# First attention: probabilities scaled in place and transposed in one pass; and three changes of the second block

## Chip, core and metric

The kernel runs on one core of one Trainium2 chip. The time is the device time of one execution, in microseconds (us). TensorE (PE) multiplies matrices, VectorE (DVE), ScalarE (ACT) and GpSimd (POOL) do the rest, and SyncE (SP) issues most transfers.

## The reference, cut to what matters

Two transformer blocks run one after the other on 512 tokens of width 1024; the second puts 16 meta tokens in front (528 rows). Only the parts that the change touches are shown.

```python
# first block: attention over three dilations, 8 heads of 64
p = jnp.exp(s - m[..., None])
l = jnp.sum(p, axis=-1)
# out = sum_i e^{m_i} o_i / sum_i e^{m_i} l_i
# second block
proj = hn_p @ w_in[l]
sb_q, sb_k, sb_v, g_q, g_k, g_v, g_r, g_lr, merge = _split_cols(proj, IN_WIDTHS)
sb = _stick_breaking(...)   # z = q.k / sqrt(d), 8 heads of 64, blocks of 128 keys
glog = jax.nn.log_sigmoid((g_lr @ w_gk_up[l] + b_gk[l])) / GATE_TAU   # g_lr: 16 columns
h = h + _rmsnorm(mix, norm_mix_post[l])
hn = _rmsnorm(h, norm_ffn_pre[l])      # _rmsnorm: y = x * rsqrt(mean(x*x) + EPS) * g
```

## The kernel before

The first block keeps the tokens on the free axis. Its attention treats two heads at once (`hp`, four pairs) and four query blocks of 128 rows each (`i`); block `i` sees `i + 1` key blocks. A software pipeline of five stages runs over these 16 units: scores (`at_scores`), maximum and exponential (`at_exp`), transposition (`at_transpose`), copy out of PSUM (`at_evac`) and the product with the values (`at_out`, which also splits the finished pair of heads into a high and a low part on ACT and DVE, L220 and L221). `at_transpose` builds the diagonal of the reciprocal sums on ACT (L708) and multiplies the exponentials by it as a float32 product (L712), which scales and transposes them. A float32 product is two matmul instructions in the trace, a product of split operands (float32r) one, a transpose one.

Beside the attention DVE works off the taps of the causal convolution (`taps`, L635), which stand at a lower priority. Behind the attention PE does the first half of the output projection (`pw`); the convolution's result `y` is completed at L861 and enters the sums of `conv_norm` (L824). Memory that the attention held becomes the buffers `raw2`; the last columns of `w_mod` are loaded there, and GpSimd multiplies two of these loads (L519).

The weights come through one stream (`ws`): a unit is loaded into a `raw` buffer, and units that are marked for it are split into a high part (ACT, L220) and a low part (DVE or GpSimd, L221). Products of split operands are three matmuls (`mm3`, L309 to L311, and L1587, L1609, L2210).

At the start of the second block DVE and ACT make the normed input `nh`/`nl` (L1655 to L1657). The gate's rank-16 projection (`w_lr`, in the pool `pl`) is one unit of 128 columns of which 16 are used; ACT copies the result to `glr` (L1718), and `decay` multiplies it by `wgk`. Then one `weave` interleaves the stick-breaking attention (`sb_gen`), the projections of queries and keys (`qk_gen`), the gated attention (`gla_gen`) and a value projection. `sb_gen` is a pipeline over 40 units (pair of heads, key block `j`, head `b`) with the stages `sb_z`, `sb_soft`, `sb_cum`, `sb_sum`, `sb_exp`, `sb_out`; a score lies in its PSUM bank `pz` from `sb_z` to `sb_exp`. All of these streams take their banks from one pool of eight.

Behind the mixing, the class `Sums` adds up squares over the channels with products by ones, for the halves `a` of the tokens: 8 squares of the mixed output (`mix_mm`, `mix_out`) and 8 of the new residual (`h_gen`, for the feed-forward part's norm). Before, each square is multiplied by a 32-column piece of ones into one of four column groups, and `rstd` copies the four partial sums out (L1640) and joins them by one more product (L1641) ahead of the logarithm (L1642).

The order of instructions on each engine is decided when the program is built, by a planner that goes by priorities and by its own estimate of durations; `high_priority` and `keep_in_program_order` steer it. A change of one stage can so move instructions of others.

Of the kernel before, what the change touches and what calls it, by code (L numbers as in the profile page):

```python
# [11 lines left out]
F32 = mybir.dt.float32  # L12
F32R = mybir.dt.float32r
I32 = mybir.dt.int32
AF = mybir.ActivationFunctionType
# [5 lines left out]
P = 128  # L21
T = 512
D = 1024
KD = D // P
# [28 lines left out]
def pack_inputs(a):  # L53
# [18 lines left out]
    def cols(w, starts):  # L72

        kk = w.shape[0] // P
        return np.stack([w[:, s:s + P].reshape(kk, P, P).transpose(1, 0, 2).reshape(P, -1) for s in starts])
# [6 lines left out]
    def pair(x):  # L82
# [7 lines left out]
    w2 = f("w_in_2")[0]  # L90
# [14 lines left out]
                           .reshape(NE, 2, P, 2048) for w in (gate, up, down)], axis=1).reshape(NE, 6, P, 2048),  # L105
        "b_r": np.concatenate([f("b_router_group").reshape(1, 4), f("b_router_expert").reshape(1, NE)], axis=1),
        "w_v2": pair(np.concatenate([rows(w2[:, c:c + 512], 2) for c in (1024, 2560, 3072)])),
        "w_lr": cols(w2, [4608]),
        "w_qk2": pair(cols(w2, [c + h * P for c, h in (
            (0, 0), (512, 0), (1536, 0), (2048, 0), (1536, 1), (2048, 1), (0, 1), (512, 1),  # L110
            (1536, 2), (2048, 2), (1536, 3), (2048, 3), (0, 2), (512, 2), (0, 3), (512, 3))])),
# [84 lines left out]
def _build(ctx, nc, tc, I, out, dbg):  # L196
    mm = nc.tensor.matmul
    transpose = nc.tensor.transpose
    act = nc.scalar.activation
# [117 lines left out]
    big = A.enter_context(tc.tile_pool(name="A", bufs=1, side="right"))  # L317
# [11 lines left out]
    ident = const.tile([P, P], F32, name="ident")  # L329
    ones = const.tile([P, P], F32, name="ones")  # L330
    nc.vector.memset(ones, 1.0)
    epsb = const.tile([P, 1], F32, name="epsb")
# [42 lines left out]
    def p1(name="p1"):  # L375
        return pp.tile([P, 512], F32, name=name, tag="p1", bufs=4)
# [9 lines left out]
    plan = []  # L386
# [71 lines left out]
    nmoe = len(plan)  # L458
    two = (1024, 1024)
    plan += [(I["w_v2"][i], two, "keep") for i in range(2)]  # L460
    plan += [(I["w_lr"][0], (1024,), True)]
    plan += [(I["w_qk2"][i], two, True) for i in range(8)]
    plan += [(I["w_v2"][i], two, "keep") for i in range(2, 6)]
    plan += [(I["w_gr"][i], two, True) for i in range(4)]
# [11 lines left out]
    ws = Stream(plan, castp, 3, nmoe)  # L476
# [57 lines left out]
    for k in range(KD):  # L534
        sq = big.tile([P, T], F32, name="sq", tag=("sq", "t512")[k % 2], bufs=2)
# [4 lines left out]
        g = slice(32 * (k % 4), 32 * (k % 4) + 32)  # L540
# [161 lines left out]
    def at_transpose(un, st):  # L702
        hp, i = un
        s, sm = st
        nc.vector.reciprocal(sm[:, 6:8], sm[:, 4:6])
        dg = big.tile([P, 2, P], F32, name="dg", tag="dg", bufs=2)
        for b in range(2):
            act(dg[:, b, :], ident, AF.Copy, scale=sm[:, 6 + b:7 + b])  # L708
        pt = [p1("pt0"), p1("pt1")]
        for b in range(2):  # L710
            for j in range(i + 1):
                mm(pt[b][:, j * P:(j + 1) * P], s[:, b, j * P:(j + 1) * P], dg[:, b, :], start=True, stop=True)  # L712
        return pt

    def at_evac(un, pt):
# [713 lines left out]
    ws = main  # L1429
# [132 lines left out]
    def t5(name, p=P):  # L1562
        return HP.tile([p, L], F32, name=name, tag="t5", bufs=4)
# [15 lines left out]
    def proj2_gen(k, xh, xl, ps):  # L1579

        wh, wl = ws.nxt(P)
        for kk in range(k):
            if kk:
                yield
            for l, r, fl in ((wh, xh, 0), (wh, xl, 1), (wl, xh, 2)):
                for a in range(2):
                    mm(ps[a], l[:, kk, :], r[kk][:, a * HF:(a + 1) * HF],  # L1587
                       start=(kk == 0 and fl == 0), stop=(kk == k - 1 and fl == 2))
# [27 lines left out]
    def part(ap, a):  # L1616
        return ap[:, E[a][0]:E[a][1]]

    class Sums:
# [9 lines left out]

        def flush(self, a):  # L1630
            for sq in self.pend[a]:
                g, k = self.n[a] % 4, self.n[a]
                mm(self.ps[a][32 * g:32 * g + 32], ones[:, 0:32], part(sq, a), start=(k < 4), stop=(k >= 4),
                   skip_group_check=True)
                self.n[a] += 1
            self.pend[a] = []

        def rstd(self, a, r, count):
            ev = t5("ev")
            act(part(ev, a), self.ps[a], AF.Copy)  # L1640
            mm(self.ps[a], ones, part(ev, a), start=True, stop=True)  # L1641
            tc.keep_in_program_order(act(part(r, a), self.ps[a], AF.Ln, bias=epsb, scale=1.0 / (32 * count)))  # L1642
            tc.keep_in_program_order(act(part(r, a), part(r, a), AF.Exp, scale=-0.5))


# [63 lines left out]
    sv = sp_.tile([P, 5, 512], F32, name="sv")  # L1709
    sv_last = vproj_end(sv, psv[:4], psv[4], t5("tail")[:, :T], psx, rcol)  # L1710
    pl = [p("pl")[:, :HF] for p in (pns, psx)]
    for i, _ in enumerate(proj2_gen(KD, nh, nl, pl)):
        if i == 2:
            sv_last()
    tc.keep_in_program_order(nc.scalar.preload_act_table_set("natural_log_exp_and_others"))
    glr = t5("glr", 16)
    for a in range(2):
        act(glr[:, a * HF:(a + 1) * HF], pl[a][0:16], AF.Copy)  # L1718
    ws.lo = tt
    PB.close()  # L1720
    PS, p1, p2 = psum_pool("psumC", 4, 2)
    wgk = cp.tile([16, 512], F32, name="wgk")
    nc.gpsimd.dma_start(wgk, I["w_gk_up"])
    resetm = cconst("resetm", L)
    cum = s8("cum")

# [43 lines left out]
    def need(*what):  # L1770
        while not made.issuperset(what):
            next(qkg)
# [7 lines left out]
    def sb_keys(j):  # L1780
        return NM if j == 4 else P

    def sb_z(un, _):
        hp, j, b = un
        need(("s", hp))
        s0, t0, n = SBT[j]
        ps = p1("pz")
        r, p = slice(64 * b, 64 * b + 64), sb_keys(j)
        mm(ps[:p, :n], skh[hp][r, s0:s0 + p], sqh[hp][r, t0:t0 + n], start=True, stop=True)  # L1789
        return ps  # L1790

    def softplus(pss, n, p=P):

# [355 lines left out]
    def mix_mm(m, a):  # L2149
        if m not in wo:  # L2150
            wo[m] = ws.nxt(P)
            sqo[m] = t5("sq")
        wh, wl = wo[m]
        ps = pso[m, a] = p1("pmix")[:, :E[a][1] - E[a][0]]
        for kk in range(KD):
            mm3(ps, wh[:, kk, :], wl[:, kk, :], part(mh[kk], a), part(ml[kk], a), kk == 0, kk == KD - 1)

    def mix_out(m, a):
        ps = pso.pop((m, a))
        act(part(mx[m], a), ps, AF.Copy, scale=cc("norm_mix_post", m))  # L2160
        act(part(sqo[m], a), ps, AF.Square)
        su.add(a, sqo[m])

    for m in range(KD - 2):
        for a in range(2):
            mix_mm(m, a)
        for a in range(2):
            mix_out(m, a)
            if m in (3, 5):
                su.flush(a)  # L2170

    for a in range(2):
        for m in (KD - 2, KD - 1):
            mix_mm(m, a)
            mix_out(m, a)
        su.flush(a)
        with tc.high_priority(offset=100):
            su.rstd(a, r, D)
# [8 lines left out]
    def h_gen(a):  # L2187
        for k in range(KD):
            with tc.high_priority(offset=200):
                t, h, g = cp.tile([P, T], F32, name="t", tag="y", bufs=3)[:, :E[a][1] - E[a][0]], part(hT[k], a), cc("norm_ffn_pre", k)  # L2190
                tt(t, part(mx[k], a), part(r, a), OP.mult)
                (nc.gpsimd.tensor_tensor if k in HPL else tt)(h, h, t, OP.add)
                act(part(nh[k], a), h, AF.Copy, scale=g)
                stt(part(nl[k], a), h, g, part(nh[k], a).bitcast(F32), OP.mult, OP.subtract)
            sq = t5("sq")
            act(part(sq, a), h, AF.Square)
            su.add(a, sq)
            if k % 2:
                su.flush(a)
            yield  # L2200

# [159 lines left out]
```

## Time and profile before

| | us |
|---|---|
| timed runs | 1836.7, 1839.62 (median), 1840.88 |
| the profiled execution | 1838.8 |
| its span, first to last instruction | 1837.0 |
| PE busy | 1752.8 (95%) |
| DVE busy | 923.4 (50%) |
| ACT busy | 626.5 (34%) |
| POOL busy | 180.4 (10%) |

The busy shares are a mean over stages with different limits; the time of a stage is set by the engine that is busy throughout it, or by a wait. PE's busy time counts matmuls whose ends are modelled, and neighbours overlap.

### The profile page before, as it was taken

How to read it: one execution, taken by the hardware profiler on the slowest of the kernel's cores; microseconds unless marked ns; L12 is line 12 of the kernel's file. 1: busy time of each engine (PE TensorE's matmuls, PEld its weight loads, DVE VectorE, ACT ScalarE, POOL GpSimd, SP SyncE). 2: the span in 40 equal slices, each digit the busy share in tenths (PEclk: the TensorE clock that was granted, in tenths of full speed). 3: DMA queues.
4: the chain of work that ended last, by engine and by line, in shares of the span. 5: the costliest groups of instructions: out<-in, count | busy, mean ns of one | idle time of the engine just before them, and what ended most of it. 6: DMA issues, size and time to landing. Idle time of an engine off the chain costs nothing.

```text
span 1837.0 us, 26718 instructions
## 1 busy us (share of the span) xinstructions
PE 1752.8 (95%) x10738; PEld 1264.7 (69%) x10738; DVE 923.4 (50%) x1593; ACT 626.5 (34%) x1146; POOL 180.4 (10%) x162
## 2 busy tenths in 40 slices
PE   6978987999999999999999999999999999999997
PEld 4755754544445444445888768989999799889985
DVE  7999864542424343335577752253331654335534
ACT  3324653211111111104566663252223633223322
POOL 4541020000000000004100000030000111001101
PEclk9998998999999999999999999999999999999998
DMA  8743163899999999941411012113222122232221
GB/s 300 283 165 134 73 231 127 303 409 409 408 411 377 371 407 409 413 166 38 157 63 47 25 38 101 47 50 136 104 95 91 46 92 93 90 105 93 92 86 63
DMA packets 73889, 328.29 MB, mean 179 GB/s; under 512 B 7971, under 2 KB 8227, under 8 KB 59556
## 3 DMA queue, kind: packets, MB, share of 16 engines
q1 hardware_dynamic: 72608, 320.75, 46.3%
q0 software_dynamic: 1152, 5.81, 0.9%
q8 instruction: 85, 1.39, 0.3%
q14 instruction: 40, 0.33, 0.1%
q10 hardware_dynamic: 4, 0.00, 0.0%
HBM read 322.27 MB, written 4.26 MB: 178 GB/s over the span
## 4 chain that ended last, share of the span: by engine, by line
PE 50%; DVE 2%; ACT 1%; POOL 1%; issue 0%; DVEq 0%; ACTq 0%; POOLq 0%
PE p L1609 11%; PE pup L2210 7%; PE pq L1587 6%; PE pg L311 2%; PE pg L309 2%; PE pg L310 2%; PE pd L310 2%; PE pd L311 2%; PE pd L309 2%; PE pz L1789 1%; PE pv L309 1%; PE psb L1870 1%; PE pv L311 1%; PE pv L310 1%; PE pmix L309 1%; PE pmix L310 1%
## 5 line engine op out<-in xcount | busy, mean ns | idle before, releaser
L221 DVE TENSOR_TENSOR wsplit<-raw,wsplit 128x1024 fp32r<-128x1024 f32 (+1 forms) x140 | 166.8, 1194 | 258.5 <-ACT wsplit L220 253.0
L220 ACT ACTIVATE wsplit<-raw 128x1024 fp32r<-128x1024 f32 (+1 forms) x145 | 147.9, 1022 | 261.8 <-PE pd L311 76.4
L1195 PE MATMUL pgu<-raw,x 128*64 128x512 f32 x960 | 220.3, 598 | 0.0
L1195 PEld LDWEIGHTS pgu<-raw,x 128*64 128x64 f32 x960 | 64.1, 136 | 120.0 <-issue 106.9
L1288 DVE SCALAR_TENSOR_TENSOR x<-psx,modc,x 128x512 f32<-128x512 f32 x136 | 93.1, 744 | 48.1 <-PE psx L1296 48.0
L1237 DVE SCALAR_TENSOR_TENSOR yl<-pdn,wsl,yh 128x512 fp32r<-128x512 f32 x34 | 25.4, 751 | 178.8 <-ACT yh L1236 178.4
L1195 PE MATMUL pdn<-raw,hT 128*64 128x512 f32 x480 | 105.7, 593 | 0.7 <-ACT hT L1217 0.7
L635 DVE SCALAR_TENSOR_TENSOR y<-u,cpk,y 128x512 f32<-128x512 f32 x116 | 103.3, 924 | 0.4
L1217 ACT ACTIVATE hT<-pht 128x512 f32<-128x512 f32 x17 | 10.2, 598 | 232.1 <-PE pht L1211 227.5
L1195 PEld LDWEIGHTS pdn<-raw,hT 128*64 128x64 f32 x480 | 34.5, 137 | 69.1 <-issue 64.4
L310 PE MATMUL pd<-wsplit,ah 128*128 128x512 f32 x176 | 71.0, 403 | 2.1 <-DVE wsplit L221 2.0
L1157 PE MATMUL psg<-oh,h2h 128*128 128x256 f32 (+1 forms) x288 | 68.9, 297 | 3.2 <-DVE oh L1142 3.2
L311 PE MATMUL pd<-wsplit,al 128*128 128x512 f32 x176 | 70.0, 398 | 0.0
L309 PE MATMUL pd<-wsplit,ah 128*128 128x512 f32 x176 | 69.1, 398 | 1.0 <-ACT wsplit L220 1.0
L1609 PE MATMUL p<-nha,wsplit 128*128 128x258 f32 x384 | 68.6, 291 | 1.0 <-ACT grb L2059 0.6
L1157 PE MATMUL psg<-oh,h2l 128*128 128x256 f32 (+1 forms) x288 | 65.7, 281 | 0.0
L1609 PE MATMUL p<-nhb,wsplit 128*128 128x258 f32 x384 | 65.5, 282 | 0.0
L221 POOL TENSOR_TENSOR wlo<-raw,whi 128x1024 fp32r<-128x1024 f32 x20 | 59.4, 2982 | 57.7 <-ACT whi L220 47.2
L2210 PE MATMUL pup<-nha,wsplit 128*128 128x258 f32 x352 | 63.9, 290 | 0.9 <-ACT wsplit L220 0.9
L523 DVE CUSTOM_DVE_ANT_0 raw<-raw,h 128x1024 f32<-128x1024 f32 x38 | 62.4, 1668 | 1.1 <-DMA raw<-w_mod 1.1
L1295 PE MATMUL psx<-ohT,yh 128*128 128x512 f32 x136 | 59.3, 436 | 3.3 <-ACT uh L1455 3.0
L2210 PE MATMUL pup<-nhb,wsplit 128*128 128x258 f32 x352 | 61.4, 284 | 0.0
(649 smaller groups left out, 4050.7 us busy)
## 6 DMA issues: line engine op xcount, KB each, us to landing
raw<-w_moe SPq DMA_DIRECT2D x312, 512.0 KB, 10.1
raw<-w_moe SPq DMA_DIRECT2D x36, 1024.0 KB, 8.9
raw<-w_mod SPq DMA_DIRECT2D x24, 1024.0 KB, 6.4
raw<-w_ff SPq DMA_DIRECT2D x22, 1024.0 KB, 4.8
raw<-w_qk SPq DMA_DIRECT2D x12, 1024.0 KB, 4.9
raw<-w_v SPq DMA_DIRECT2D x8, 1024.0 KB, 4.9
raw<-w_mg SPq DMA_DIRECT2D x8, 1024.0 KB, 4.8
raw<-w_fd SPq DMA_DIRECT2D x8, 1024.0 KB, 4.8
```

What stands on the lines that cost most here:

```text
L220: act(hi, src, AF.Copy)
L221: return sub(lo, src, hi.bitcast(F32), OP.subtract)
L309: mm(ps, lh, rh, start=first, stop=False)
L310: mm(ps, lh, rl, start=False, stop=False)
L311: mm(ps, ll, rh, start=False, stop=last)
L635: tap[0] = stt(y[:, m, :], src, w, y[:, m, :], OP.mult, OP.add)
L1157: fix(mm(ps[k // 2][:, k % 2 * 256:][:, :n], w[i][:, k * P:(k + 1) * P], oh[:, i, :n], start=(i == 0 and w is h2h and k % 2 == 0), stop=(i ...
L1195: fix(mm(ps[s, :], l[:, s], w[:, 2 * b + i, :], start=first, stop=last, skip_group_check=True))
L1288: stt(xT[m], ps, gt2(m), xT[m], OP.mult, OP.add)
L1587: mm(ps[a], l[:, kk, :], r[kk][:, a * HF:(a + 1) * HF], start=(kk == 0 and fl == 0), stop=(kk == k - 1 and fl == 2))
L1609: mm(ps[a], l[:, kk, :], ends(r[kk])[:, a], start=(kk == 0 and fl == 0), stop=(kk == k - 1 and fl == 2))
L2210: mm(ps[:, a, :HC], l[:, kk, :], x[kk][:, o:o + HC], start=(kk == 0 and fl == 0), stop=(kk == KD - 1 and fl == 2))
```

## The change

Four edits. The probabilities are scaled in place on ACT and then transposed by PE's transpose instead of multiplied by a diagonal. The rank-16 projection loads 32 columns per 128 rows (16 used, 16 zero) without a split and runs as float32 products in four column groups; the four partial results are kept, and `wgk` holds the 16 rows four times, with zeros between, so that the decay product adds them up. The two heads' scores of a key block are issued together. `Sums` multiplies by the full square of ones, one square at a time and one step later, so that nothing has to be joined.

```diff
@@ pack_inputs
-        "w_lr": cols(w2, [4608]),
+        "w_lr": np.pad(w2[:, 4608:4624], ((0, 0), (0, 16))).reshape(KD, P, 32).transpose(1, 0, 2).reshape(1, P, KD * 32),
@@ the stream's plan
-    plan += [(I["w_lr"][0], (1024,), True)]
+    plan += [(I["w_lr"][0], (KD * 32,), False)]
@@ at_transpose
-        dg = big.tile([P, 2, P], F32, name="dg", tag="dg", bufs=2)
+        n = (i + 1) * P
         for b in range(2):
-            act(dg[:, b, :], ident, AF.Copy, scale=sm[:, 6 + b:7 + b])
+            act(s[:, b, :n], s[:, b, :n], AF.Copy, scale=sm[:, 6 + b:7 + b])
...
-                mm(pt[b][:, j * P:(j + 1) * P], s[:, b, j * P:(j + 1) * P], dg[:, b, :], start=True, stop=True)
+                transpose(pt[b][:, j * P:(j + 1) * P], s[:, b, j * P:(j + 1) * P], ident)
@@ Sums
             for sq in self.pend[a]:
-                g, k = self.n[a] % 4, self.n[a]
-                mm(self.ps[a][32 * g:32 * g + 32], ones[:, 0:32], part(sq, a), start=(k < 4), stop=(k >= 4),
-                   skip_group_check=True)
+                mm(self.ps[a], ones, part(sq, a), start=(self.n[a] == 0), stop=(self.n[a] == KD - 1))
...
         def rstd(self, a, r, count):
-            ev = t5("ev")
-            act(part(ev, a), self.ps[a], AF.Copy)
-            mm(self.ps[a], ones, part(ev, a), start=True, stop=True)
-            tc.keep_in_program_order(act(part(r, a), self.ps[a], AF.Ln, bias=epsb, scale=1.0 / (32 * count)))
+            tc.keep_in_program_order(act(part(r, a), self.ps[a], AF.Ln, bias=epsb, scale=1.0 / count))
@@ the rank-16 projection
-    for i, _ in enumerate(proj2_gen(KD, nh, nl, pl)):
-        if i == 2:
+    w = ws.nxt(32)
+    for k0 in (0, 4):
+        for x in (nh, nl):
+            for a in range(2):
+                for k in range(4):
+                    mm(pl[a][32 * k:32 * k + 32], w[:, k0 + k, :], x[k0 + k][:, a * HF:(a + 1) * HF].bitcast(F32),
+                       start=(k0 == 0 and x is nh), stop=(k0 > 0 and x is nl), skip_group_check=True)
+        if k0 == 0:
             sv_last()
...
-    wgk = cp.tile([16, 512], F32, name="wgk")
-    nc.gpsimd.dma_start(wgk, I["w_gk_up"])
+    wgk = cp.tile([P, 512], F32, name="wgk")
+    nc.gpsimd.memset(wgk, 0.0)
+    for g in range(0, P, 32):
+        nc.gpsimd.dma_start(wgk[g:g + 16], I["w_gk_up"])
@@ sb_z
+        if b == 0:
+            need(("s", hp))
+            s0, t0, n = SBT[j]
+            p = sb_keys(j)
+            for h in range(2):
+                pz[h] = p1("pz")
+            for h in range(2):
+                r = slice(64 * h, 64 * h + 64)
+                mm(pz[h][:p, :n], skh[hp][r, s0:s0 + p], sqh[hp][r, t0:t0 + n], start=True, stop=True)
+        return pz.pop(b)
@@ mixing
         for a in range(2):
             mix_mm(m, a)
+            su.flush(a)
         for a in range(2):
             mix_out(m, a)
-            if m in (3, 5):
-                su.flush(a)
...
         for m in (KD - 2, KD - 1):
             mix_mm(m, a)
+            su.flush(a)
             mix_out(m, a)
@@ h_gen
             act(part(sq, a), h, AF.Square)
+            su.flush(a)
             su.add(a, sq)
-            if k % 2:
+            if k == KD - 1:
                 su.flush(a)
```

## Rows read from the trace of the kernel before

**Rows 1.** Windows of the first attention, of what follows: engines' busy us, clock, DMA.
```profile
168.00:221.70 53.70, 46.14 (x358) 34.06 (x354) 49.75 (x131) 38.01 (x116) 1.56 (x1) 0.94 0.12 41
222.00:240.00 18.00, 12.59 (x42) 7.65 (x41) 17.20 (x13) 5.59 (x10) 9.65 (x3) 0.95 0.84 335
```

**Rows 2.** Timeline behind the attention: start, us, engine, line, operation, idle before it.
```profile
222.05 0.69 DVE L221 TENSOR_TENSOR ml<-pso,mh 128x512 fp32r<-128x512 f32 x1 [2.22 <-ACT mh L220]
226.15 6.50 DVE L635 SCALAR_TENSOR_TENSOR y<-u,cpk,y 128x512 f32<-128x512 f32 x3
226.47 4.84 POOL L519 TENSOR_TENSOR raw<-raw,u 128x2048 f32<-128x2048 f32 x1 [47.83 <-DMA raw<-w_mod]
241.37 2.08 PE L824 MATMUL psl<-y,ones 128*128 128x512 f32 x2 [6.78 <-DVE y L861]
```

**Rows 3.** Window of the stick-breaking and gated attention: PE, PEld, DVE, ACT, POOL.
```profile
896.00:1064.00 168.00, 166.67 (x1876) 130.92 (x1876) 114.92 (x251) 112.31 (x253) 4.17 (x8) 0.99 0.14 47
```

**Rows 4.** Timeline of PE: products with a diagonal; four transposes elsewhere, the next matmul.
```profile
188.56 2.05 PE L712 MATMUL pt<-dg,s 128*128 128x128 f32 x16
...
265.40 0.66 PE L806 MATMUL pth<-ident,xs 128*128 128x128 f32 x4
265.82 0.48 PE L309 MATMUL pw<-mh,whi 128*128 128x512 f32 x1
```

**Rows 5.** Groups by line and shape, 144 to 222 us: busy, mean ns, idle before.
```profile
L635 DVE SCALAR_TENSOR_TENSOR y<-u,cpk,y 128x512 f32<-128x512 f32 x69 | 51.0, 766 | 0.2
...
L708 ACT ACTIVATE dg<-ident,sm 128x128 f32<-128x128 f32 x32 | 11.1, 393 | 5.1 <-DVE sm L705 3.3 <-DVE sm L697 1.8
...
L699 ACT ACTIVATE s<-s,sm 128x512 f32<-128x512 f32 x8 | 5.7, 712 | 4.3 <-DVE sm L697 4.3
```

**Rows 6.** Timeline of the norm and the rank-16 projection at the second block's start.
```profile
868.37 2.41 POOL L221 TENSOR_TENSOR wsplit<-raw,wsplit 128x1024 fp32r<-128x1024 f32 x1 [0.15 <-ACT wsplit L220]
869.18 3.98 DVE L1657 TENSOR_TENSOR nla<-nt,nha 128x512 fp32r<-128x512 f32 x4
...
878.85 0.69 DVE L1657 TENSOR_TENSOR nlb<-nt,nhb 128x512 fp32r<-128x512 f32 x1
...
881.23 0.65 ACT L1718 ACTIVATE glr<-pl 16x264 f32<-16x264 f32 x2 [1.30 <-PE pl L1587]
...
883.40 2.36 DVE L221 TENSOR_TENSOR wsplit<-raw,wsplit 128x1024 fp32r<-128x1024 f32 x2
```

**Rows 7.** Score products: their busy time in one window (PE, PEld), then the timeline.
```profile
896.00:1064.00 168.00, 26.40 (x80) 9.99 (x80) 0.99 0.14 47
...
918.50 0.94 PE L1789 MATMUL pz<-sqk 64*128 64x400 f32 x2
...
937.42 1.12 PE L1789 MATMUL pz<-sqk 64*128 64x512 f32 x2
938.47 0.51 PE L1587 MATMUL pq<-nhb,wsplit 128*128 128x264 f32 x2
...
1059.97 0.94 PE L1789 MATMUL pz<-sqk 64*128 64x400 f32 x4
...
1062.31 1.56 PE L1789 MATMUL pz<-sqk 64*128 64x512 f32 x4
```

**Rows 8.** Sums of squares: windows (partial sums alone; all engines), then PE's timeline.
```profile
1396.00:1456.00 60.00, 14.27 (x64) 3.39 (x64) 0.94 0.16 53
...
1426.00:1436.00 10.00, 7.20 (x23) 3.13 (x22) 9.03 (x22) 8.38 (x21) 2.80 (x3) 0.68 0.00 0
...
1420.55 0.67 PE L1641 MATMUL psum<-ev,ones 128*128 128x260 f32 x2
...
1421.17 0.28 PE L309 MATMUL pmix<-mhb,wsplit 128*128 128x256 f32 x1
...
1428.93 0.62 PE L1633 MATMUL psum<-sq,ones 128*32 128x256 f32 x2 [1.86 <-ACT sq L2161]
1430.02 1.22 PE L1641 MATMUL psum<-ev,ones 128*128 128x256 f32 x2 [0.47 <-ACT ev L1640]
```

More of the change, by code (lines that the diff above doesn't have):

```diff
@@ L1711, in _build @@
     pl = [p("pl")[:, :HF] for p in (pns, psx)]
-    for i, _ in enumerate(proj2_gen(KD, nh, nl, pl)):
-        if i == 2:
+    w = ws.nxt(32)
[6 more added lines that the diff above has]
+        if k0 == 0:
             sv_last()
     tc.keep_in_program_order(nc.scalar.preload_act_table_set("natural_log_exp_and_others"))
-    glr = t5("glr", 16)
+    glr = t5("glr")
     for a in range(2):
-        act(glr[:, a * HF:(a + 1) * HF], pl[a][0:16], AF.Copy)
+        act(glr[:, a * HF:(a + 1) * HF], pl[a], AF.Copy)
     ws.lo = tt
@@ L1781, in sb_keys @@
         return NM if j == 4 else P
+    pz = {}
     def sb_z(un, _):
         hp, j, b = un
[L1785 to L1790, printed above, removed]
+        if b == 0:
[8 more added lines that the diff above has]
+        return pz.pop(b)
     def softplus(pss, n, p=P):
```

## Prediction

> **What bounds the kernel now.** A saving on TensorE (PE) counts only in a stage that waits for PE, so I read the busy time of all engines by window first, then the timeline at the places where PE stands still.
>
> In the first attention it is not PE. From 168 to 221.7 us VectorE (DVE) is busy 49.75 of 53.70 us, and 17.20 of 18.00 us behind it [rows 1]. It does the attention's reductions and, between them, the convolution taps. Past the attention PE stands 6.78 us until DVE has finished the convolution (L861) [rows 2]. Whatever PE does sooner in the attention is added to that wait, except for time in which DVE itself had nothing to do: 53.70 - 49.75 = 3.95 us in the attention and 0.80 us behind it. The longest piece is 2.22 us, the wait for the last head's output (L221 on ACT) [rows 2].
>
> In the second block it is PE: 166.67 of 168 us busy in the stick-breaking and gated-attention stage, with DVE at 114.92 and ACT at 112.31 [rows 3]. There a PE saving is a time saving as long as other matmuls are ready.
>
> **Part 1, probabilities.** Removed: 160 matmul instructions against a diagonal (4 head pairs, 10 blocks, 2 halves, each float32 product two instructions). Sixteen took 2.05 us, 0.128 each, so 20.5 us. Added: 80 transposes. Four transposes began at 265.40 and the next matmul at 265.82 [rows 4], 0.105 each, so 8.4 us. PE loses 12.1 us of work. ACT: 32 diagonals of 393 ns (11.1 us busy together) become 32 in-place scalings. For 128 columns I price them at the same 393, for 512 at the exponential's 712 [rows 5], between by a line (499, 606): 8 x 2.21 = 17.7 us, so ACT gains at most 6.6 us on 38.01 busy of 53.70 [rows 1] and stays below DVE. DVE's work is unchanged. So 12.1 us go off PE and at most 3.95 + 0.80 = 4.75 us come out. I take -2.5: the wait of 2.22 for the last head goes, little else. Bounds: -4.75, and +3, if the taps are ordered worse around the two GpSimd products that follow. While one of these runs (4.84 us from 226.47) three taps take 6.50 us [rows 2], against 766 ns for a mean tap [rows 5]; both products hit DVE wherever the taps stand, and a third one caught would cost some 4.2 us, less the 1 to 2 us of idle recovered.
>
> **Part 2, the gate's rank-16 projection.** Removed: 48 matmuls, and the split of their weight on ACT and GpSimd. Added: 32 float32 products of 32 columns, four at a time in four column groups. But the stage follows a norm chain on DVE: the last piece of its input (L1657) is made from 878.85 to 879.54, and the products end at 881.23, where ACT copies them [rows 6]. So the end moves by two small terms. First, the GpSimd split of this weight (868.37 to 870.78) overlaps four subtractions on DVE that take 3.98 us; at the 0.69 of the one that stands alone they would take 2.76 [rows 6], and 1.2 us go. Second, behind the last piece come two of the eight groups of four products; half a microsecond for a group is an estimate from a full-array float32 product of 260 columns (0.50, part 4), since the four run side by side: 1.0 instead of the 1.7 there now. Sum -1.9. Against it: the first product of the next projection needs a weight half that DVE splits from 883.40 on [rows 6], behind six other updates, and that moves only with the first term. I take -1.4, bounds 0 and -3. The added memset and three DMA issues stand on GpSimd's queue ahead of the reset mask; the first decay that reads it comes more than 10 us later, which hides them, and without that cover they cost their length, some 2 us.
>
> **Part 3, score pairs.** The 40 score products are 80 instructions, 26.40 us busy [rows 7]. Each uses 64 of the 128 rows, and 36 of them stand alone in the stream; only the last head's two largest pairs stand together (0.94 and 1.56 us). So 23.9 us are singles. A single of 512 columns is 1.12 us busy, but the next matmul begins 1.05 behind its start (937.42, 938.47): 0.07 of each is overlap, and 36 singles hold PE for 23.9 - 36 x 0.07 = 21.4 us. A pair of 400 columns takes 0.94 us, a single of 400 columns also 0.94 [rows 7]: the second half is free. So half of 21.4 goes, 10.7 us. PE has other matmuls in hand there, and DVE and ACT are at 67 to 68% [rows 3], so I take -9; bounds -10.7 and -3, the rest for banks (below).
>
> **Part 4, sums of squares.** Removed: four copies (ACT) and four products that joined the four partial sums. The 32 partial sums (14.27 us busy; with four joins of 0.67, 17.0) become 32 full-array products [rows 8]. A join of 260 columns is such a product: it begins at 1420.55, and the matmul after the next one at 1421.17, one slot of 0.12 after 1421.05, so it holds PE for 0.50. 32 x 0.50 = 16.0, so -1.0 on PE; with the busy time of a partial sum (0.45) it is -2.7, with that of a join (0.67) +4.4. More lies in one place: from 1426 to 1436 PE is busy 7.20 of 10.00 us at a mean clock of 0.68 [rows 8]. It waits 1.86 us for a square, then the join waits 0.47 for the copy and takes 1.22 at the lower clock. Without copy and join some 1.7 us of that chain go, and about 1 us of the same chain one half earlier. I take -2.7 there and -3.7 together; bounds -7 and +1.7.
>
> **The sum.** -2.5 - 1.4 - 9 - 3.7 = -16.6. The profiled execution took 1838.8 us (span 1837.0 and 1.8 around it), 0.8 below the median of the three timed runs, 1839.62. 1838.8 - 16.6 = 1822.2; I say 1822.
>
> **Rivals.**
> *Banks run out (slower).* A pair takes both its PSUM banks one unit early, and eight banks serve scores, projections and outputs. If PE's next instruction is a second score without a bank, it waits for the exponential of a unit four steps back, and all that is queued behind it on PE waits too. A step lasts 168 / 40 = 4.2 us; half a step at 18 pairs is 38 us, against 10.7 saved: 1838.8 - 7.6 + 27 = 1858. It turns to a loss once a pair waits 0.6 us. For it: five scores would be held at the peak instead of four. Against it: PE idles only 1.3 us in the stage now [rows 3], and two pairs already stand together. [...]
>
> [...]
>
> *The second block gives half.* Its filler is not ready, or ACT sets the pace of the last head: parts 2 to 4 give -7 rather than -14.1, the time is 1838.8 - 9.5 = 1829.
>
> **How the numbers follow.** Forecast 0.70, half 0.12, clock 0.10, banks 0.08. The forecast's own range, from the bounds of the parts, is 1812 to 1831; the range reaches to the half and the clock case and leaves the banks out: 1812 to 1833. A measurement of this kernel can tell 0.2%, 3.7 us. Faster by more than that: forecast, half, and less than half of the clock case (partly worse than worked out), 0.86; within it 0.06; slower: the banks, 0.08.
>
> **What would show it.** Part 1 right: DVE as busy as now up to the end of the convolution, PE's wait there longer than 6.78 us, the convolution done 2 to 3 us sooner; wrong: DVE idle more, or L861 later. Part 2: the products end about 1 us behind the last DVE subtraction. Part 3: 20 groups of four score instructions with about half of 26.40 us, and no new waits before them; a wait for an exponential in front of a score is the bank rival. Part 4: no copy and no join, and the low-clock stretch between mixing and feed-forward shorter by 2 us. [...]

## The result, and the profile after

The changed kernel takes 1827.45 us, the median of 6 runs (1825.18 to 1828.79); the kernel before took 1838.13 in as many runs on the same chip. The ratio is 0.9942, with a 95% interval of 0.9930 to 0.9953: 10.7 us faster. The prediction was 1822, with a range of 1812 to 1833. The profiled execution took 1827.8 us (span 1826.0 and 1.8 around it), 11.0 below that of before.

Where these 11.0 us come from is read from PE's timeline, from one landmark to the next: the first product of `psk` (L1018, behind the router), the last transpose of `pht` (L1211, the end of the experts), the first product of `pq` (L1587, behind the rank-16 projection), the first transpose of `pkt` (behind the stick-breaking and gated attention), and the end of the span.

| stage, us | before | after | difference | part |
|---|---|---|---|---|
| start to `psk` | 314.0 | 314.4 | +0.4 | 1 |
| `psk` to last `pht` | 507.0 | 506.2 | -0.8 | none |
| last `pht` to `pq` | 62.7 | 62.5 | -0.2 | 2 |
| `pq` to `pkt` | 241.0 | 233.9 | -7.1 | 3 |
| `pkt` to the end | 712.3 | 709.0 | -3.3 | 4 |

First the windows of the changed kernel that answer to [rows 1] and [rows 3] (PE, PEld, DVE, ACT, POOL busy, granted clock, DMA):

```profile
168.00:221.70 53.70, 42.77 (x298) 26.52 (x295) 48.40 (x130) 41.83 (x113) 1.56 (x1) 0.94 0.14 42
222.00:240.00 18.00, 13.04 (x45) 7.97 (x43) 17.20 (x14) 6.52 (x10) 10.28 (x3) 1.00 0.94 386
896.00:1064.00 168.00, 163.48 (x1907) 130.89 (x1908) 122.15 (x266) 117.75 (x274) 10.39 (x18) 0.98 0.14 48
```

In the attention PE is relieved, DVE is idle for 5.30 us where it was 3.95, and ACT has grown from 38.01 to 41.83. The next rows, the timeline behind the attention, answer to [rows 2]:

```profile
220.65 0.69 DVE L221 TENSOR_TENSOR ml<-pso,mh 128x512 fp32r<-128x512 f32 x1 [1.49 <-ACT mh L220]
221.26 2.32 DVE L635 SCALAR_TENSOR_TENSOR y<-u,cpk,y 128x512 f32<-128x512 f32 x3
...
224.74 6.51 DVE L635 SCALAR_TENSOR_TENSOR y<-u,cpk,y 128x512 f32<-128x512 f32 x3
...
231.77 0.75 DVE L635 SCALAR_TENSOR_TENSOR y<-u,cpk,y 128x512 f32<-128x512 f32 x1
...
233.03 8.05 DVE L635 SCALAR_TENSOR_TENSOR y<-u,cpk,y 128x512 f32<-128x512 f32 x5
...
225.00 4.91 POOL L519 TENSOR_TENSOR raw<-raw,u 128x2048 f32<-128x2048 f32 x1 [45.77 <-DMA raw<-w_mod]
...
233.17 5.01 POOL L519 TENSOR_TENSOR raw<-raw,u 128x2048 f32<-128x2048 f32 x1 [0.60 <-DMA raw<-w_mod]
...
242.89 2.07 PE L824 MATMUL psl<-y,ones 128*128 128x512 f32 x2 [7.85 <-DVE y L861]
```

The last head is split 1.4 us sooner, but 12 taps stand behind it instead of 8, both GpSimd products again stand across them, and PE's wait for the convolution is longer than before (7.85 against 6.78) and ends later (242.89 against 241.37).

The groups by line and shape from 144 to 222 us show what part 1 changed in work. Of the kernel before:

```profile
L712 PE MATMUL pt<-dg,s 128*128 128x128 f32 x160 | 24.0, 300 | 9.9 <-ACT dg L708 5.0 <-ACT qk L667 4.9
```

Of the changed kernel:

```profile
L712 PE MATMUL pt<-ident,s 128*128 128x128 f32 x80 | 14.2, 305 | 11.0 <-ACT s L708 6.3 <-ACT qk L667 4.7
...
L708 ACT ACTIVATE s<-s,sm 128x512 f32<-128x512 f32 x8 | 5.3, 715 | 0.7 <-DVE sm L705 0.7
...
L708 ACT ACTIVATE s<-s,sm 128x384 f32<-128x384 f32 x8 | 4.5, 608 | 1.2 <-DVE sm L705 1.1
...
L708 ACT ACTIVATE s<-s,sm 128x256 f32<-128x256 f32 x8 | 3.6, 503 | 1.5 <-DVE sm L697 0.9 <-DVE sm L705 0.6
...
L708 ACT ACTIVATE s<-s,sm 128x128 f32<-128x128 f32 x8 | 2.8, 395 | 2.1 <-DVE sm L705 2.1
```

PE loses 9.8 us. ACT's 32 scalings take 16.2 us where the diagonals took 11.1 [rows 5], and PE's waits for L708 grow from 5.0 to 6.3 us.

The rank-16 projection (now L1712, its copies L1719, the norm's pieces L1652), to set beside [rows 6]:

```profile
868.62 1.90 DVE L1652 TENSOR_TENSOR nla<-nt,nha 128x512 fp32r<-128x512 f32 x3
...
877.65 0.69 DVE L1652 TENSOR_TENSOR nlb<-nt,nhb 128x512 fp32r<-128x512 f32 x1 [0.31 <-ACT nhb L1651]
878.26 4.69 DVE L1655 SCALAR_TENSOR_TENSOR x<-x,cpk,pspread 128x512 f32<-128x512 f32 x7
882.87 2.36 DVE L221 TENSOR_TENSOR wsplit<-raw,wsplit 128x1024 fp32r<-128x1024 f32 x2
...
879.31 0.39 ACT L1719 ACTIVATE glr<-pl 128x264 f32<-128x264 f32 x1 [1.11 <-PE pl L1712]
...
880.54 0.38 ACT L1719 ACTIVATE glr<-pl 128x264 f32<-128x264 f32 x1
...
883.10 0.48 PE L1587 MATMUL pq<-nha,wsplit 128*128 128x264 f32 x2 [1.08 <-DVE x L1655]
```

The last piece is made 1.2 us sooner. Of the two copies, which stood together from 881.23 to 881.88, the first now starts 1.9 us sooner; the second stands behind the split of a weight and ends 1.0 us sooner (880.92). The next projection starts only 0.6 sooner, for it waits for DVE's seven updates. About 0.4 us of all this comes from ahead of the stage: the last `pht` is that much sooner too.

The scores (now L1799), to set beside [rows 7]: their busy time in the window, then PE's timeline, of one pair and of the end of the stage.

```profile
896.00:1064.00 168.00, 16.73 (x80) 5.77 (x80) 0.98 0.14 48
```

```profile
934.22 1.13 PE L1799 MATMUL pz<-sqk 64*128 64x512 f32 x4
...
1042.92 0.27 PE L1951 MATMUL pat<-gf 128*16 128x16 f32 x4 [0.50 <-ACT z L1866]
...
1051.54 0.39 PE L1904 MATMUL pc<-sp,c_tge 16*16 16x128 f32 x2 [0.78 <-DVE sp L1901]
...
1052.25 1.65 PE L1799 MATMUL pz<-sqk 64*128 64x512 f32 x2
1053.83 0.74 PE L1880 MATMUL psb<-z,sv 128*64 128x144 f32 x2
1054.50 2.07 PE L1799 MATMUL pz<-sqk 64*128 64x512 f32 x2
```

26.40 us have become 16.73. A pair of 512 columns takes 1.13 us, where a single one took 1.12 [rows 7]. The last four instructions take 3.7 us, where the same four took 1.56 before, for two reasons: PE runs at the lower clock there (mean 0.59 from 1052 to 1056 us), and a product of `psb` stands between the two halves, so that they don't run together. The row of `pat` shows a product of the gated attention that reads no exponential and yet waits 0.50 us for one; what holds it can only be the bank that the exponential reads.

The sums of squares (L1632), to set beside [rows 8]: a window of all engines, then PE's timeline.

```profile
1420.00:1430.00 10.00, 7.69 (x43) 6.21 (x43) 10.00 (x23) 9.18 (x25) 2.38 (x3) 1.00 0.00 0
```

```profile
1423.14 2.02 PE L1632 MATMUL psum<-sq,ones 128*128 128x256 f32 x8 [2.07 <-ACT sq L2171]
...
1429.12 0.71 PE L1632 MATMUL psum<-sq,ones 128*128 128x260 f32 x2 [0.24 <-ACT sq L2206]
```

The wait for the square is still there (2.07 us, 1.86 before), the copy, the join and their 1.69 us are gone, and the stretch at a mean clock of 0.68 is at 1.00. DVE is busy for all of these 10 us: it is the bound there now.

### The profile page after: what moved, and what is told of

Its sections match the earlier page's. It is cut to its first block, busy times and chain, and to the rows that moved or that the text cites. A ratio compares the mean times of both kernels' runs of the same rounds, so it can differ in the third digit from the quotient of the medians.

```text
span 1826.0 us, 26562 instructions
## 1 busy us (share of the span) xinstructions
PE 1732.1 (95%) x10666; PEld 1252.3 (69%) x10666; DVE 923.6 (51%) x1593; ACT 627.3 (34%) x1141; POOL 181.9 (10%) x165
## 4 chain that ended last, share of the span: by engine, by line
PE 47%; DVE 4%; ACT 2%; DMA 1%; POOL 1%; issue 1%; DVEq 0%; ACTq 0%; POOLq 0%
PE p L1609 11%; PE pup L2221 7%; PE pq L1587 4%; PE pg L311 2%; PE pg L309 2%; PE pg L310 2%; PE pd L310 2%; PE pd L311 2%; PE pd L309 2%; PE pv L309 1%; PE pv L311 1%; PE pv L310 1%; PE pmix L309 1%; PE pmix L311 1%; PE pmix L310 1%; PE psb L1880 1%
## 5 line engine op out<-in xcount | busy, mean ns | idle before, releaser
L2221 PE MATMUL pup<-nha,wsplit 128*128 128x258 f32 x352 | 62.7, 287 | 0.4 <-ACT wsplit L220 0.4
L523 DVE CUSTOM_DVE_ANT_0 raw<-raw,h 128x1024 f32<-128x1024 f32 x38 | 62.5, 1671 | 0.8 <-DMA raw<-w_mod 0.8
```

The costliest lines, as they stand in the source:

```text
L2221: mm(ps[:, a, :HC], l[:, kk, :], x[kk][:, o:o + HC], start=(kk == 0 and fl == 0), stop=(kk == KD - 1 and fl == 2))
```

## The experiments

Every kernel was timed beside the kernel before on the same chip; the ratios are to it, with 95% intervals.

| run | ratio | interval | median, us |
|---|---|---|---|
| changed kernel | 0.9942 | 0.9930 to 0.9953 | 1827.45 |
| e1, part 1 alone | 1.0006 | 0.9992 to 1.0020 | 1837.93 |
| e2, parts 2 to 4 | 0.9944 | 0.9930 to 0.9958 | 1828.13 |
| e3, 64 taps left out, diagonals | 0.9959 | 0.9945 to 0.9974 | 1831.11 |
| e4, 64 taps left out, transposes | 0.9961 | 0.9946 to 0.9975 | 1830.94 |
| e5, part 3 alone | 0.9950 | 0.9935 to 0.9964 | 1830.10 |
| e6, part 4 alone | 0.9989 | 0.9980 to 0.9998 | 1836.29 |
| e7, two GpSimd products to DVE | 0.9906 | 0.9888 to 0.9925 | 1821.60 |
| e8, gated attention spread | 0.9945 | 0.9924 to 0.9966 | 1826.48 |
| e9, e7 and eight taps on PE | 0.9897 | 0.9882 to 0.9913 | 1821.32 |
| e10, e7 with diagonals | 0.9899 | 0.9881 to 0.9916 | 1819.41 |
| e11, e4 with the scaling on DVE | 0.9923 | 0.9906 to 0.9940 | 1825.14 |
| e12, e9 and the third product to DVE | 0.9898 | 0.9881 to 0.9914 | 1817.70 |

### What each part is worth: e1, e2, e5, e6

e1 is the kernel before with the hunk of `at_transpose`; e2 is the changed kernel with that hunk undone; e5 has the hunk of `sb_z` alone; e6 the hunks of `Sums`, of the mixing and of `h_gen`. The diffs are those of the section on the change.

> The kernel before with the change of the first attention alone. Theory (VectorE bounds this stage): the 12 us that TensorE saves go into its wait for the convolution, the convolution ends no sooner (240.6 us before, 242.2 in the changed kernel), and the time is that of the kernel before, 1837 to 1840 us. Rival (the step of the prediction holds, -2.5 us, and the second block fell short by more): 1835 to 1836, the convolution done at about 238.

Measured: 1.0006. Part 1 alone gives nothing that the runs can tell: at most 1.5 us of gain lie in the interval. The rival, -2.5 us, falls.

> The changed kernel without the change of the first attention: the three changes of the second block alone. Theory (VectorE bounds the attention): as fast as the changed kernel, 1826 to 1828 us, or a little faster, since the convolution ends 1.5 us sooner without it. Rival (the attention gave 2.5 us): 1830.

Measured: 0.9944 against 0.9942 with part 1. Within the intervals all of the gain is made by parts 2 to 4. This pair alone would not exclude the rival; e1 does.

> The kernel before with the two heads' scores issued together, nothing else. Theory (this part carries two thirds of the gain): the stick-breaking stage ends 7 us sooner, the time is 1830 to 1832 us, and its end shows a stretch at the lower clock that the kernel before does not have. Rival (the gain is made by other parts and banks eat this one): 1834 or more.

Measured: 0.9950, -9.2 us (-6.6 to -12.0). In its trace `pq` to `pkt` takes 233.8 us, 7.2 less than before, and the end of the stage shows the lower clock (0.94 mean from 1020 to 1060 us, 1.00 before). All three points of the theory came. This part carries most of the gain.

> The kernel before with the full-array sums of squares alone. Theory: 4 us, of which the two joins and the copies at the low clock are 3; the time is 1833 to 1835 us, and the stretch between mixing and feed-forward shows no clock below 0.9. Rival (the sums gain on TensorE but the chain of square, logarithm and update sets the time there): 1837 to 1838.

Measured: 0.9989, -2.0 us (-0.4 to -3.7). The interval reaches into both expectations, 3 to 5 us less and at most 1 us less, and decides for neither. In the trace `pkt` to the end takes 707.0 us, 5.3 less, but `pq` to `pkt`, in which nothing was changed, 1.5 more. The mean clock from 1430 to 1440 us is 0.84, so "no clock below 0.9" was wrong for this kernel.

Set over several traces, the stages give one size for each part:

```
stage, us           without the part                 with it                      difference
part 1, to psk      314.0 (before) 315.2 (e2)        314.4 (after) 314.0 (e1)
                    314.5 (e5) 313.9 (e6)            314.5 (e8)                   -0.1
part 2, pht to pq   62.7 (before) 63.2 (e1)          62.5 (after) 61.5 (e2)
                    62.5 (e5) 62.6 (e6)              61.6 (e8)                    -0.9
part 3, pq to pkt   241.0 (before) 239.5 (e1)        233.9 (after) 233.1 (e2)
                    242.5 (e6)                       233.8 (e5)                   -7.4
part 4, pkt to end  712.3 (before) 712.3 (e1)        709.0 (after) 708.9 (e2)
                    710.4 (e5)                       707.0 (e6)                   -3.4
```

A stage in which nothing differs scatters by up to 4.4 us from kernel to kernel, so the last column is good to about 1 us. The rows leave out the traces of kernels that were changed elsewhere. With them part 3 is the same, but part 4 is smaller: `pkt` to the end takes 710.9, 709.4 and 707.9 us without it in e3, e4 and e11, and 705.9 to 709.1 with it in e7 to e10 and e12, so that the means of all traces differ by 2.6. The experts (`psk` to last `pht`), in which nothing was changed, take 506.1 to 507.2 us in all traces.

### Why the attention gives nothing: e3, e4, e11

The prediction said that DVE's taps hide what PE saves. If so, the saving must appear once the taps are fewer.

```diff
-            for j in range(31 if m < 3 else 31 - NPT):
+            for j in range(15 if m < 3 else 15 - NPT):
```

> The kernel before with 15 taps instead of 31 for each of the four convolution groups; the 64 others, some 49 us of VectorE work at 0.77 us, are left out of the computation. This is the base for the next run. Both theories: VectorE is no longer the bound behind the attention, the wait of 6.8 us for the convolution goes, and the time falls by 7 us or more, to about 1830.

> The same 64 taps left out, with the probabilities scaled in place and transposed. Theory (TensorE did get 12 us shorter, VectorE hid it): now it shows, 8 to 12 us less than the run with the diagonals, about 1820. Rival (the scaling in place lengthens the chain of each unit, exponential, scaling, transposes, copy, and eats what TensorE saves): the same time as the run with the diagonals, within 2 us.

Measured: 0.9959 and 0.9961. The theory, 8 to 12 us, falls; the rival's time, the same within 2 us, is the one measured. Its reason is not shown by this. With DVE busy for only 6 of 19 us the last pair of heads is split at the same time in both. Timeline of DVE, e3 and then e4:

```profile
217.41 0.69 DVE L221 TENSOR_TENSOR ml<-pso,mh 128x512 fp32r<-128x512 f32 x1 [6.08 <-ACT mh L220]
```

```profile
217.37 0.69 DVE L221 TENSOR_TENSOR ml<-pso,mh 128x512 fp32r<-128x512 f32 x1 [6.32 <-ACT mh L220]
```

What holds e4 there can be ScalarE: from 196 to 215 us it is busy 16.97 of 19 us, with PE at 17.25 and DVE at 5.60. From 168 to 222 us PE's matmuls wait 0.3 us in e3 and 4.2 in e4, 3.5 of these for copies by ScalarE (`qk`, L667, and `pT`, L720). So the scaling was moved to the idle engine:

```diff
-            act(s[:, b, :n], s[:, b, :n], AF.Copy, scale=sm[:, 6 + b:7 + b])
+            ts(s[:, b, :n], s[:, b, :n], sm[:, 6 + b:7 + b], None, OP.mult)
```

> The run with 64 taps left out and the transposes, with the scaling of the probabilities moved from ScalarE to VectorE, which is idle for 33 of 52 us there. Theory (with VectorE free the chain through ScalarE sets the pace: exponential, scaling, copy, 33.8 us busy of 39): ScalarE loses 16 us, the last pair of heads is split 4 us or more before 217.4 us. Rival (the length of a unit's chain does not matter, TensorE's fixed work does): the last split stays at 217 us.

Measured: 0.9923, some 7 us less than e4 by the ratios, and the intervals do not touch. Of the 5.0 us between the two traces 3.8 lie ahead of `psk` (307.6 to 303.8) and 1.5 behind `pkt`, where the kernels are equal. The split moves by 3.2 us, a little less than the 4 expected. A window and the timeline of e11:

```profile
196.00:215.00 19.00, 18.04 (x137) 12.39 (x137) 9.09 (x32) 10.84 (x33) 0.00 (x0) 1.00 0.03 6
```

```profile
214.18 0.69 DVE L221 TENSOR_TENSOR ml<-pso,mh 128x512 fp32r<-128x512 f32 x1 [4.47 <-ACT mh L220]
```

The rival ("the last split stays at 217 us") falls. But the run does not show that ScalarE sets the pace of the whole stage. The units with four key blocks, one for each pair of heads, begin their products into `pt` at these times:

```
                      1st      2nd      3rd      4th
e3, diagonals         173.98   186.56   199.36   212.30
e4, scaling on ACT    173.51   188.81   201.06   212.45
e11, scaling on DVE   173.88   186.09   198.09   209.46
```

From the second to the fourth e4 needs 23.6 us, e11 23.4 and e3 25.7: there transposing does gain some 1 us for each pair of heads, and it hardly matters which engine scales. Nearly all of e4's delay against e11, and more than all against e3, arises between the first and the second. There ScalarE is busy in e4 for 13.96 of the 16 us from 172 to 188 (13.52 in e3, 11.85 in e11), PE waits 2.12 us for its copy `qk` (1.12 in e11), and the clock falls, which it does in neither of the others (1.00 from 172 to 180 us in e3 and e11). Windows and timeline of e4, then the timeline of e11:

```profile
172.00:176.00 4.00, 2.49 (x12) 1.65 (x12) 1.45 (x7) 3.86 (x11) 0.00 (x0) 0.75 0.66 210
176.00:180.00 4.00, 4.00 (x24) 2.27 (x24) 1.27 (x7) 2.81 (x11) 0.00 (x0) 0.82 0.50 204
```

```profile
173.51 1.54 PE L712 MATMUL pt<-ident,s 128*128 128x128 f32 x8 [2.12 <-ACT qk L667]
174.98 1.22 PE L686 MATMUL pqk<-qk 64*128 64x256 f32 x4
176.14 1.48 PE L729 MATMUL pso<-pT,vt 128*64 128x128 f32 x12
```

```profile
173.88 1.09 PE L712 MATMUL pt<-ident,s 128*128 128x128 f32 x8 [1.12 <-ACT qk L667]
174.90 0.70 PE L686 MATMUL pqk<-qk 64*128 64x256 f32 x4
175.53 0.88 PE L729 MATMUL pso<-pT,vt 128*64 128x128 f32 x12
```

The same three groups take 4.24 us in e4 and 2.67 in e11, so the clock can account for some 1.6 of the 3.2 us, and ScalarE's work for the rest; the two were not tried apart. That e3 and e4 end together at 217.4 is then chance: a late start and a faster pace cancel. And e11, with ScalarE and DVE both relieved, splits only 3.2 us before the diagonals of e3, and its `psk` starts 0.9 us sooner (303.8 against 304.7). Where the rest of PE's saving goes stays open.

### What stands behind the attention: e7, e10, e9, e12

```diff
-    NMP = (15, 21, 23)
+    NMP = (15,)
```

> The changed kernel with two of GpSimd's three products (those behind the attention) done by VectorE as the others are: 4 x 1.21 us more on VectorE. Theory (a GpSimd product of 128x2048 stops VectorE for about 4 us of its 4.9): the taps that took 6.5 us for three and 8.05 us for five take 0.77 each, 8.5 us come back against 4.8 us of new work, the convolution ends about 3.5 us sooner and the time falls by 2 to 4, to 1824. Rival (the loads that arrive then, at a mean DMA share of 0.84, slow VectorE): the taps stay slow, the convolution ends 4.8 us later, 1830 or more.

Measured: 0.9906, 6 to 7 us less than the changed kernel by the ratios, more than the 2 to 4 expected. Of the 7.9 us between the two traces 4.5 lie ahead of `psk`, where the products stand; 2.4 lie between `pq` and `pkt`, where e7's trace lacks a dip of the clock (below). The timeline of DVE:

```profile
229.96 2.32 DVE L635 SCALAR_TENSOR_TENSOR y<-u,cpk,y 128x512 f32<-128x512 f32 x3
...
234.85 3.89 DVE L635 SCALAR_TENSOR_TENSOR y<-u,cpk,y 128x512 f32<-128x512 f32 x5
...
239.81 0.68 DVE L861 TENSOR_TENSOR y<-pyt,y 128x512 f32<-128x512 f32 x1
```

Three taps take 2.32 us and five 3.89 while the loads still arrive (DMA share 0.91 to 1.01): the rival falls. The convolution ends 2.3 us sooner and `psk` starts 4.5 us sooner. PE hardly waits for it any more (0.6 us, in front of a weight load), and that is in spite of a new cost: the clock. Windows of e7 behind its last transposes:

```profile
212.00:216.00 4.00, 2.51 (x20) 1.85 (x20) 3.96 (x7) 3.46 (x8) 0.00 (x0) 0.90 0.00 0
216.00:220.00 4.00, 4.00 (x20) 3.60 (x18) 2.41 (x4) 1.19 (x2) 0.00 (x0) 0.50 0.00 0
...
224.00:228.00 4.00, 4.00 (x10) 3.05 (x10) 2.03 (x3) 0.00 (x0) 0.00 (x0) 0.50 0.94 381
```

PE is busy for 2.51 of 4 us at 212 us, then runs at a granted clock of 0.50 until 228 us, and the last head is split at 223.18 instead of 220.65.

> The run with the two GpSimd products on VectorE, but with the diagonals in the first attention. It asks what transposing is worth once VectorE is relieved. Theory (the chain of a unit through ScalarE and VectorE ends the attention, not TensorE): the same time as with transposes, 1820 to 1823; the denser products with the diagonal hold the clock at 1.0 behind 212 us, where the transposes left it at 0.5 for 13 us, and this may make it up to 3 us faster. Rival (TensorE is the bound once VectorE is relieved, and its 9.8 us come back): 1827 or more.

Here `at_transpose` is that of the kernel before, all else is e7. Measured: 0.9899 against 0.9906: the same within the intervals. Part 1 is worth nothing that the runs can tell with DVE relieved, too, and the rival, 1827 or more, falls. Why is not shown by this pair: the chain through ScalarE and the lower clock of e7 both stand against the transposes. In e10 the clock is 1.00 in all windows from 196 to 260 us; one of them:

```profile
224.00:228.00 4.00, 4.00 (x19) 3.21 (x18) 3.37 (x6) 0.63 (x1) 0.00 (x0) 1.00 0.98 322
```

In this pair of traces `psk` starts 3.0 us sooner with the diagonals (306.9 against 309.9). The timed runs do not confirm it.

```diff
-    NPT = 4
+    NPT = 8
```

> The changed kernel, two GpSimd products moved to VectorE as in the run before, and eight instead of four of the convolution's taps done by TensorE. Theory (VectorE's convolution still ends last behind the attention): four taps of 0.77 us leave VectorE, TensorE takes 3.6 us more in time that it has, 1 to 3 us less than without, 1819 to 1821. Rival (with the GpSimd products gone TensorE is the bound there, it was busy 18.0 of 18 us behind the attention): 3.6 us of new TensorE work, 1824 to 1826.

Measured: 0.9897, within the interval of e7, as good as the theory asks (-1.7 us by the ratios) but not told apart from no change. The rival, 3.6 us more, falls. In the trace `psk` starts at 307.9, 2.0 sooner than in e7, and PE does all eight products of L824 without a wait.

> The run with eight taps on TensorE and two GpSimd products on VectorE, with the third product, the one at 125 us, moved as well. Theory (each GpSimd product of 128x2048 costs VectorE some 4 us and 2.4 us on VectorE itself, and VectorE is full from 140 to 168 us): 1.5 us less, 1819 to 1820 us. Rival (there the TensorE's value projection sets the pace, VectorE's taps are not awaited): the same, 1821.

The edit is `NMP = ()`. Measured: 0.9898 against 0.9897 for e9: the 1.5 us can't be told apart from nothing by the timed runs. In its trace `psk` starts 3.5 us sooner (304.4 against 307.9), which speaks for the theory; this stays open.

e7, e9, e10 and e12 beat both kernels: about 1.0% below the kernel before. e9 is the changed kernel with two constants changed, and its interval (0.9882 to 0.9913) lies below that of the changed kernel (0.9930 to 0.9953).

### What the pairs of scores lost: e8

```diff
-    weave((sb_gen(), 0, 1), (qkg, 0, 0.33), (gla_gen(), 6.6, 1.6), (sb_meta(), 32.5, 1.6),
+    weave((sb_gen(), 0, 1), (qkg, 0, 0.33), (gla_gen(), 6.6, 2.0), (sb_meta(), 32.5, 1.6),
```

> The changed kernel with the gated attention spread wider in the weave (a step every 2.0 units instead of 1.6), so that its products last until the last scores. Theory (the pairs used up the filler, and TensorE's 3 us of idle and the low clock behind 1040 us are the price): these go, 2 to 4 us less, 1824. Rival (the chain of the last units through ScalarE and VectorE sets the end of the stage): 1827 to 1829, the idle time moves but stays.

Measured: 0.9945, the changed kernel's 0.9942. The low clock at the end is gone, but not the idle time, and `pq` to `pkt` takes 235.9 us instead of 233.9. One place where it loses is the stage's start: the first scores wait 2.5 us for ScalarE's copy `sqk` (L1761), 1.4 in the changed kernel. The window of the stage's end in the kernel before, there also over the 40 us as far ahead of its later `pkt` as in the changed one, then in the changed kernel, e7 and e8:

```profile
1020.00:1060.00 40.00, 39.18 (x568) 25.64 (x566) 30.88 (x74) 28.79 (x73) 1.89 (x5) 1.00 0.01 2
1027.70:1067.70 40.00, 38.59 (x542) 23.67 (x542) 30.79 (x82) 31.81 (x81) 1.57 (x4) 1.00 0.01 2
```

```profile
1020.00:1060.00 40.00, 36.88 (x532) 22.01 (x529) 29.68 (x82) 32.49 (x82) 3.10 (x4) 0.91 0.01 2
```

```profile
1020.00:1060.00 40.00, 36.88 (x508) 22.94 (x507) 32.23 (x85) 36.41 (x88) 3.10 (x4) 1.00 0.01 2
```

```profile
1020.00:1060.00 40.00, 37.23 (x560) 23.04 (x559) 33.91 (x90) 32.38 (x80) 3.67 (x4) 1.00 0.01 2
```

PE idles some 3 us in all three kernels with pairs, and 1.4 in the kernel before over the same part of the stage. The theory falls, and the rival's forecast came: the idle time stays. For its reason speak the waits of PE's matmuls from 1000 to 1075 us, which are all for steps of ScalarE and VectorE: 3.0 us in the changed kernel, 2.5 in e8, 1.4 before. Of the 3.0 us 1.7 are for a unit's operands (`ahi` 0.8, `alo` 0.4, `z` 0.5), 0.8 for the meta tokens (`sp`), and 0.5 is the wait of `pat` for a bank. In e8 two products wait in this way for an exponential that they don't read, 0.69 and 0.55 us. In e7 the clock stays at 1.00 and the stage takes 231.5 us (1109.3 - 877.8), 9.5 less than before; in the six traces with these pairs and a mean clock below 0.95 there it takes 233.1 to 234.6. So the dip costs some 2 us, an estimate from these times. Pairs are not its only cause: a smaller one stands at about the same place in e6 (0.83 from 1060 to 1070 us, where the changed kernel has 0.66 from 1050 to 1060) and in e11 (0.97 from 1010 to 1060), which have none. What keeps it away in e7 was not tried.

## Why the prediction was right, and where its steps failed

The forecast held in sign and range: faster, inside 1812 to 1833. It was 5.4 us too low, half of that in part 1, and the measured time lies nearer to the rival "the second block gives half" (1829, chance 0.12) than to 1822. The range was kind: 1812 to 1831 is said to come from the bounds of the parts, but these add up to 1813.4 on one side and 1840.5 on the other.

**The bound.** Right: behind the attention PE waits for DVE, and a saving on PE goes into that wait [rows 2]. Not enough: DVE is not the only reason. With 64 taps less the saving was still gone (e3, e4); with the scaling off ScalarE, too, the last split came 3.2 us sooner (e11), of which the clock may have made half.

**Part 1, -2.5, measured 0 (+3.7 to -1.5).** PE's saving was mis-sized, 9.8 us instead of 12.1: eight transposes take 1.09 us in the attention, where four within dense products had given 0.105 each [rows 4]. ACT's growth was bounded well (5.1 of at most 6.6 us). A step that failed is the one that dismissed it, that ACT gains 6.6 us on 38.01 of 53.70 "and stays below DVE": a mean share does not say when PE waits for ScalarE, and in e4, with DVE relieved, it waited 3.5 us for it. The other failed step is "the wait of 2.22 for the last head goes, little else": it became 1.49, the attention ended 1.4 us sooner, and four more taps stood behind it. Both signs of being wrong that the prediction named for this part came: DVE idles more (5.30 us, 3.95 before) and L861 is later. The bound of +3 for "the taps are ordered worse" was the right mechanism: L861 starts 1.5 us later. That the time did not suffer is PE's doing, which used the longer wait for eight products that stood behind it before (from 232.6 to 235 us).

**Part 2, -1.4, measured -0.9.** The first term came: the four subtractions take 2.58 us instead of 3.98, and the last piece is made 1.2 us sooner. The four products of a group ran side by side, as estimated: the eight instructions of one group begin 0.45 us behind those of the group before (873.65, 874.10), where a single instruction is 0.39 us busy. The second term came for the first copy only (1.9 us sooner, the sum); the second copy ends 1.0 us sooner, and 0.4 us of both were won ahead of the stage. What holds the next projection was named in part: it waits for the updates of `x`, seven of them now, but not for the weight half that DVE splits behind them. In both kernels it starts (883.73 and 883.10) before that split can be done (it begins at 883.40 and 882.87, 1.2 us for each half).

**Part 3, -9, measured -7.4 by the stages and -9.2 by the timed runs.** The free second half is there: 26.40 us became 16.73, 9.7 less against the 10.7 forecast. What is missing stands in part at the stage's end: 1.7 us more idle over the 40 us shown, and in all traces with pairs but e7 and e8 a dip of the clock (mean 0.91 to 0.94) that cost some 2 us by the same estimate. That PE's filler is used up there is the reading of the waits, not shown by a run; e8 moved the filler and gained nothing. The prediction left 1.7 us "for banks"; no wait of PE in front of a score is for an exponential (the one there is, 1.4 us, is for the copy `sqk`). The banks cost little, but not nothing: 0.5 us in front of `pat`.

**Part 4, -3.7, measured -3.4 by the table, -2.6 over all traces, and -2.0 by the timed run of e6.** The chain lost its copy and its join (1.69 us) and in the changed kernel the low-clock stretch; in e8, with the same sums, the clock is 0.83 from 1420 to 1430 us, so that stretch is not gone for good. The 64 instructions are 18.87 us busy, 1.9 more than the 17.0 of before, where the prediction had 1.0 less, within its bounds. But busy time counts what neighbours overlap: four products in a row hold PE for 2.02 us, 0.505 each, the 0.50 of the prediction. What the products cost in time is not shown.

**The rivals.** *Banks run out*: hardly. One product that is no score waits 0.5 us for an exponential, where the rival had 2.1 us for each of 18 pairs. *The clock*, with a chance of 0.10 and a part in the upper end of the range: no run shows the time that this case stood for. In the changed kernel the granted clock of the attention was 0.94, as before. In e7, where the transposes met a relieved DVE, it was 0.50 from 216 to 228 us, and in e9 it fell for about 4 us (mean 0.59 from 196 to 200 us). With the diagonals it stayed at 1.00 from 196 to 260 us (e10). That the transposes bring it down is not shown by this: in the changed kernel, with the same 80 transposes, it is 1.00 from 212 to 232 us. *The second block gives half*: it gave -10.3 in e2, between the -14.1 of the forecast and the -7 of this rival, with more waits for ScalarE and VectorE at the stage's end (3.0 us, 1.4 before) as the rival's second reason would have them.

## What to carry to other kernels

Before a saving on one engine is booked, take the next two engines' chains one unit at a time: here work taken off TensorE was put on ScalarE, in the same chain, and what follows the stage began no sooner with VectorE in the way, nor with about half of its taps gone. Ask of an operation on GpSimd what VectorE does meanwhile: two products moved to the fuller engine brought 4.5 us in their own stage, where the whole change had brought 10.7. Where two score products share the array the second was free (1.13 us for a pair of 512 columns, 1.12 for one), but 9.7 us less of busy time made the stage only 7.4 shorter.

## What the hardware showed that was not expected

In e3 and e4 a GpSimd product of 128x2048 held up the VectorE operation that it met, a large one and a small one by about the same time. Timeline of DVE, e3 and e4, each beside such a product (4.54 us from 229.23, 5.03 us from 230.00):

```profile
229.75 5.11 DVE L523 CUSTOM_DVE_ANT_0 raw<-raw,u 128x1024 f32<-128x1024 f32 x1
```

```profile
230.67 4.37 DVE L502 TENSOR_TENSOR modc<-macc,cpk 128x2 f32<-128x2 f32 x1
```

The first takes 1.21 us elsewhere, the second, of two columns, 0.16. The losses, 3.9 and 4.2 us, are nearly the same for 1024 columns and for two, and the operations end 1.1 and 0.0 us behind the GpSimd products (234.86 and 233.77, 235.04 and 235.03). Why the one holds up the other is not shown by the runs.

The clock fell in stretches of an otherwise equal stage: to 0.50 from 216 to 228 us in e7, where it is 1.00 in the changed kernel with the same products, and for the last scores, from 1050 to 1060 us, to a mean of 0.66 in the changed kernel and 0.74 in e5, where it is 1.00 in e7. Before these falls PE had been idle for parts of some microseconds (2.51 of 4 us busy in e7; 3.22 of 4 us from 1048 to 1052 us in the changed kernel). That alone does not tell: in the changed kernel PE is busy 2.52 of 4 us from 212 to 216 us, too, and the clock stays at 1.00. At the end of the scores the fall cost some 2 us by the estimate above, and in e7 the last head came 2.5 us later: enough to hide or feign a part of this change.
